# A hybrid decoder block: key norms by products with a block of ones, and one table load by name for each head group

## The chip, the cores and the metric

The kernel runs on one core of a Trainium2 chip. The metric is the device time of one execution in microseconds (us); before the change it is 1561.46, the median of three runs (1561.0 to 1561.86). The core's engines run side by side and wait for each other by semaphores: TensorE (PE) multiplies matrices into PSUM, VectorE (DVE) and ScalarE (ACT) work element by element, GpSimd (POOL) does the same more slowly, and SyncE (SP) starts transfers.

## The reference, cut to what matters

16 meta tokens are put ahead of 256 tokens (272 in all, width 2048, float32). One layer computes RWKV-7 time mixing and FoX attention (16 heads of 64 each) from one projection, merges both by gates, and then applies a SwiGLU network.

```python
proj = xn @ w_in                                  # RWKV, FoX and gate columns
# RWKV, per head of 64:
kk = heads(k * k_k)
kk = kk / jnp.maximum(jnp.sqrt(jnp.sum(kk * kk, axis=-1, keepdims=True)), 1e-12)
y = _wkv7_scan(rh, dh, kh, vh, -kk, kk * ah)      # decay, keys, values, -kk, kk * a
# FoX, per head of 64, _rms being x * rsqrt(mean(x * x) + 1e-6) * gain:
q = _rms(q.reshape(B, L, FOX_HEADS, HEAD_DIM), q_g)
k = _rms(k.reshape(B, L, FOX_HEADS, HEAD_DIM), k_g)
sc = jnp.einsum('bqhd,bkhd->bhqk', q, k) * ATTN_SCALE + forget_bias   # then causal softmax
```

The change concerns the two key norms: `kk` of RWKV, and `k` of FoX.

## The kernel before

All large products are made with float32r operands, each number being split into a high half and the rest: `ACT` copies the raw weights to `wh`, DVE subtracts to get `wl` (`wload`, L322 and L323), and PE multiplies `wh` with both halves of the activations and `wl` with the high half (`mm3`, or `mm2` with two halves side by side). Raw, high and low tiles have four buffers each. A load holds 1024 columns; `run` issues a load and then the products of the load before it.

The heads are worked off in four groups of four heads. A group projects RWKV's `k`, `v` and `r`, makes decay and gate terms from a low-rank product (two Sigmoids of ACT), projects FoX's `q`, `k` and `v`, and then two tiles of the branch gates (`zg`). Features lie on the 128 partitions (two heads, `m` = 0, 1 for the two pairs) and tokens along the free dimension. Everything else of a group (norms, decay, the recurrence over four chunks, the triangular solves in 112 lanes, attention) runs as background streams: Python generators that `yield` the number of nanoseconds of projection after which their next stage is due. `slot` counts projected time and puts one due stage between two k-tiles; the constants at the top (`Y_SQ`, `N_SUM` and the like) are these delays. PE's order is that of the program. For ACT, DVE, POOL and SP the framework arranges the instructions, but for stretches under `manual_schedule`, which keep the program's order.

Key norms before: `head_sums` multiplies the squares (`sq`, stationary) with `bsum`, two columns that mark the two heads, in full float32 (`pe_mm`, L355), so that tokens come to lie on partitions, in three tiles of tokens (128, 128 and 16). DVE puts a floor under the sums and refines a reciprocal root by Newton steps on 12 or 20 columns (`rsqrt_steps`, L259 to L268). `spread` has ACT repeat each root 64 times (L603), and PE transposes the result back to the features' layout (`pe_tr`, L359); DVE multiplies it in. The tiles are `ss` and `kx` in RWKV, `fss` and `fx` in FoX. The query's norm stays in the tokens' layout, since it only scales rows of the scores. RWKV's bonus term already makes a product of the wanted kind: `bs` (L789), the two halves of a split tile against `bones`, a 128x128 block matrix of ones in float32r, whose result has each head's sum on all of its 64 rows.

ACT works with one set of function tables at a time; a load puts another in place. Before, there are two loads in a group: ahead of the Sigmoids (L655), and ahead of the decay's exponentials (L706).

Of the kernel before, what the change touches and what calls it, by code (L numbers as in the profile page):

```python
# [18 lines left out]
P = 128  # L19
# [45 lines left out]
LERP = 2800  # L65
BIAS = 7000
STEP = 1000
NORM = 4200
SUMS = 2000
X_RS = 1400  # L70
X_SPREAD = 1400
X_V = 1900
X_SC = 1600
X_EXP = 1100
X_DIV = 2600
X_PT = 1400
Y_SQ = 1400
Y_SPREAD = 3300
Y_KK = 2900
Y_DECAY = 1400  # L80
Y_AB = 4400
Y_MAT = 2900
Y_NEXT = 2300
Y_BONUS = 1200
# [13 lines left out]
def hybrid_block(ctx, tc, A, out, dbg=None):  # L98
# [69 lines left out]
    xhl = xp.tile([P, KT, 2, L], F32R, tag="xhl", name="xhl")  # L168
    xh, xl = xhl[:, :, 0, :], xhl[:, :, 1, :]
    rsb = xp.tile([P, L], F32, tag="rsb", name="rsb")  # L170


    lo_pool = tc.tile_pool(name="lo", bufs=1, reuse_waits="tile")
# [31 lines left out]
    def zt_(name):  # L205
        return rw.tile([P, 274], F32, tag="z", name=name, bufs=ZB)
# [68 lines left out]
    def rstd1():  # L275
        parts = [et(f"{n}1").bitcast(F32R) for n in ("xqh", "xql")]
        split(*parts, xsum)

        def back():
            ps = aux_ps("rms1")[:, :L]  # L280
            for i in range(4):
                nc.tensor.matmul(ps, allones, parts[i % 2][:, i // 2, :], start=i == 0, stop=i == 3)
            ms = zt_("ms1")[:, :L]
            nc.vector.tensor_scalar(ms, ps, 1.0 / D, RMS_EPS, op0=ALU.mult, op1=ALU.add)
            rt = zt_("rt1")[:, :L]
            rsqrt_small(None, rsb, ms, rt, None)
        return back
# [65 lines left out]
    def pe_mm(out_, lhsT, rhs, start, stop, skip=False):  # L353
        clock[2] += 4 * max(lhsT.shape[-1], rhs.free_size()) / 2.4
        nc.tensor.matmul(out_, lhsT, rhs, start=start, stop=stop, skip_group_check=skip)  # L355
# [223 lines left out]
        nc.vector.tensor_scalar(eps1, rs1, RMS_EPS, None, op0=ALU.mult)  # L579
        gate_done.append(1)  # L580

    def tiles(n):
        return [(n - T, P), (n - P, P)] + ([(0, NMETA)] if n > T else [])

    def head_sums(dst, sqs, n, name):


        ps = aux_ps(name)  # L590
        if n > T:
            nc.gpsimd.memset(dst, 1.0)
        for i, (t0, w) in enumerate(tiles(n)):
            for m in range(2):
                c = 4 * i + 2 * m
                pe_mm(ps[:w, c:c + 2], sqs[m][:, t0:t0 + w], bsum, start=True, stop=True)
        return [(dst[:w, 4 * i:4 * i + 4], ps[:w, 4 * i:4 * i + 4]) for i, (_, w) in enumerate(tiles(n))]

    def spread(rs, m, n, name):

        tl = tiles(n)
        ex = et(name).rearrange("p m t -> p (m t)")[:, :3 * P].rearrange("p (i c) -> p i c", c=P)
        nc.scalar.activation(ex[:, :len(tl), :].rearrange("p i (h d) -> p i h d", h=2),  # L603
                             rs.rearrange("p (i m h) -> p i m h", m=2, h=2)[:, :, m, :].unsqueeze(3).to_broadcast(
                                 [P, len(tl), 2, HD]), AF.Copy)

        def back():
            ps = aux_ps(name)[:, :n]
            for i, (t0, w) in enumerate(tl):
                pe_tr(ps[:, t0:t0 + w], ex[:w, i, :], ident[:w, :w])  # L610
            return ps
        return back


    def rwkv_jobs(g):
        c0 = g * 256
        box = {"done": []}
        for nm in ("k", "v", "r"):
            box[nm] = et(f"{nm}{g}")
        jobs = []  # L620

        def post(nm, off, full):
            def f(pss):
                for m in range(2):
                    mc = vc("mu", off // P + g * 2 + m)
                    dst = box[nm]
                    lerp(pss[m], P, mc, dst[:, m, :] if full else dst[:, m, :T], full, box["done"])
            return f

        for nm, off, full in (("k", 1024, True), ("v", 2048, True), ("r", 0, False)):  # L630
            n0, n = (0, L) if full else (14, T + 2)
            jobs += cm_jobs(w_in[:, off + c0:off + c0 + 256], KT, xhl, n0, n, post(nm, off, full), name=f"{nm}{g}")


        def load():
            cs_ = slice(c0, c0 + 256)
            return wload([(96, 0, [2, 256], [((ALL, 0), A["rwkv_w2"][0][:, cs_]), ((ALL, 1), A["rwkv_a2"][0][:, cs_])]),
                          (P, 512, [2, 256], [((ALL,), kblock(A["rwkv_g2"][0][:, cs_]))])], 1024)

        def mul(w):  # L640
            (uh, ul), (gh, gl) = w
            gg = box["gg"] = ot(f"gg{g}")
            for m in range(2):
                ms = slice(m * P, (m + 1) * P)
                ps = main_ps(f"g{g}{m}")[:, :T]
                for k in range(2):
                    mm3(ps, gh[:, k, ms], gl[:, k, ms], sgh[:, k, :], sgl[:, k, :], k == 0, k == 1)
                nc.vector.tensor_copy(gg[:, m, :], ps)
            for nm, i, dh, dl, bname in (("sig", 0, twh, twl, "w0"), ("aa", 1, adh, adl, "a0")):
                dst = box[nm] = et(f"{nm}{g}")  # L650
                for m in range(2):
                    ms = slice(m * P, (m + 1) * P)
                    ps = (aux_ps if i == 0 else main_ps)(f"{nm}{g}{m}")[:, :L]
                    mm3(ps, uh[:, i, ms], ul[:, i, ms], dh, dl, True, True)
                    nc.scalar.activation(dst[:, m, :], ps, AF.Sigmoid, bias=vc(bname, 2 * g + m))  # L655
            spawn(rwkv_bg(g, box), HOP)
        jobs.append((load, mul))
        return jobs

# [10 lines left out]
    def rwkv_bg(g, box):  # L670
# [14 lines left out]
            nc.scalar.activation(kk[:, m, :], kr[:, m, :], AF.Copy, scale=vi("k_k", m))  # L685
        nc.scalar.activation(sq, kk, AF.Square)
        yield Y_SQ
        kn_ = rw.tile([P, 12], F32, tag="kn", name=f"kn{g}", bufs=2)
        kr_ = rw.tile([P, 12], F32, tag="kn", name=f"kr{g}", bufs=2)
# [5 lines left out]
        for m in range(2):  # L695
            nc.vector.tensor_tensor(kk[:, m, :], kk[:, m, :], backs[m](), op=ALU.mult)
        yield Y_KK

        cs = et(f"cs{g}")
# [279 lines left out]
    def fox_jobs(g):  # L979
# [3 lines left out]
        vv = fx.tile([P, 2, L], F32, tag="vv", name=f"vv{g}", bufs=1)  # L983
        jobs = []
        ready = []
        hs = fx.tile([P, 20], F32, tag="hs", name=f"hs{g}", bufs=4)
        hr = fx.tile([P, 20], F32, tag="hs", name=f"hr{g}", bufs=4)
        done = []

        def sums(sqs, dst, n):  # L990
            c = slice(0, 8) if dst is qn else slice(8, 20)
            for i, (d, ps) in enumerate(head_sums(hs[:, c], sqs, n, f"fss{g}{n}")):
                nc.vector.tensor_scalar(d, ps, 1.0 / HD, eps1[:d.shape[0], i:i + 1], op0=ALU.mult, op1=ALU.add)
            done.append(1)
            return
            yield

        def norms():
            while len(done) < 2:
                yield  # L1000
            yield from rsqrt_steps(fx, hr, hs, [P, 20], "ht")
            yield X_RS

            nc.vector.tensor_tensor(hs[:, 0:8], hs[:, 0:8], hr[:, 0:8], op=ALU.mult)
            backs = [spread(hr[:, 8:20], m, L, f"fx{g}{m}") for m in range(2)]
            yield X_SPREAD
            for m in range(2):
                nc.vector.tensor_tensor(kn[:, m, :], kn[:, m, :], backs[m](), op=ALU.mult)
            yield
            ready.append(1)  # L1010

        def post(dst, n):
            def f(pss):
                sqs = []
                for m in range(2):
                    ps = pss[m]
                    if dst is vv:
                        nc.scalar.activation(dst[:, m, :], ps[:, :n], AF.Copy)
                        continue
                    sq = fx.tile([P, L], F32, tag="sqf", name=f"sqf{g}", bufs=3)  # L1020
                    if dst is qn:
                        halves(dst[:, m, :], ps)
                        nc.scalar.activation(sq[:, :n], dst[:, m, :], AF.Square)
                    else:
                        nc.scalar.activation(sq[:, :n], ps[:, :n], AF.Square)
                        nc.scalar.activation(dst[:, m, :], ps[:, :n], AF.Copy, scale=qk8)
                    sqs.append(sq)
                if dst is vv:
                    spawn(fox_bg(g, qn, kn, vv, hs, hr, ready), HOP)
                else:  # L1030
                    spawn(sums(sqs, dst, n), SUMS)
                    if dst is kn:
                        spawn(norms(), PREP)
# [5 lines left out]
    def fox_bg(g, qn, kn, vv, hs, hr, ready):  # L1039
# [13 lines left out]
        while not ready or not gate_done:  # L1053
# [338 lines left out]
```

## Time and profile before

| | us |
|---|---|
| median of three runs | 1561.46 (1561.0 to 1561.86) |
| the profiled execution | 1561.2 |
| its span, first to last instruction | 1559.5 |
| PE busy | 1552.3 |
| weight loads of PE (PEld) busy | 1365.3 |
| DVE busy | 1013.9 |
| ACT busy | 765.8 |
| POOL busy | 98.5 |

The clock granted to TensorE was 1.000 over the span. In a row of the timeline the first number is the start from the span's first instruction, the second the duration, both in us, and `x12` is the number of instructions in the row; a full-precision product is recorded as two, so six products of `head_sums` are `x12`. Matmuls follow each other before the one ahead has ended, so the time that one takes from the next is read from start to start and not from its duration. In a row of groups the numbers behind the bar are the busy time in us and the mean duration in ns, then the idle time of the engine ahead of it and what ended it. A row of a stretch gives the stretch, its length, the busy time of PE, PEld, DVE, ACT and POOL with their instructions, the clock, the share of the DMA engines and GB/s.

### The profile page before, as it was taken

What the parts mean: (1) busy time and instruction counts of PE and PEld (TensorE: products, weight loads), DVE (VectorE), ACT (ScalarE), POOL (GpSimd) and SP (SyncE); (2) the same over time, 40 slices, a digit from 0 to 9 for tenths busy, and PEclk for the clock granted to TensorE, in tenths of its full rate; (3) what the DMA queues carried; (4) which work ended last, traced back from release to release, by engine and by line L of the source; (5) the groups of instructions that cost most, each with busy time, mean ns of one, the idle gap of its engine ahead of it and who ended that gap; (6) DMA issues with size and microseconds to landing.
All of it is one profiled execution on the core that took longest, in us unless ns stands there. A gap on an engine that the chain in (4) does not pass through costs nothing.

```text
span 1559.5 us, 26189 instructions
## 1 busy us (share of the span) xinstructions
PE 1552.3 (100%) x10225; PEld 1365.3 (88%) x10225; DVE 1013.9 (65%) x1854; ACT 765.8 (49%) x1118; POOL 98.5 (6%) x194
## 2 busy tenths in 40 slices
PE   9999999999999999999999999999999999999998
PEld 9999998989989888999888888888888888888887
DVE  7878688677767856875665666566556666444443
ACT  7655455464555544653544555455445544333332
POOL 2121103102203100000000000000000000000000
PEclk9999999999999999999999999999999999999999
DMA  8656546546644656767566666666666665666663
GB/s 269 179 151 172 158 132 173 159 117 174 172 136 138 182 171 197 245 222 238 181 184 180 189 187 191 187 188 187 187 188 187 187 190 188 188 201 202 185 201 102
DMA packets 211483, 283.33 MB, mean 182 GB/s; under 512 B 23888, under 2 KB 128352, under 8 KB 211360
## 3 DMA queue, kind: packets, MB, share of 16 engines
q1 hardware_dynamic: 206752, 277.53, 60.4%
q10 hardware_dynamic: 4608, 4.13, 0.8%
q8 instruction: 80, 1.31, 0.4%
q14 instruction: 43, 0.35, 0.1%
HBM read 274.43 MB, written 7.19 MB: 181 GB/s over the span
## 4 chain that ended last, share of the span: by engine, by line
PE 95%; DVE 3%; DMA 1%; ACT 1%; issue 1%; SPq 0%; DVEq 0%; ACTq 0%
PE up L392 10%; PE gt L392 10%; PE zg L392 7%; PE dn L1255 5%; PE dn L1254 5%; PE dn L1253 5%; PE up L394 5%; PE gt L394 5%; PE zg L394 3%; PE f L333 2%; PE f L392 2%; PE f L335 2%; PE f L334 2%; PE br L334 2%; PE br L335 2%; PE br L333 2%
## 5 line engine op out<-in xcount | busy, mean ns | idle before, releaser
L323 DVE TENSOR_TENSOR wl<-raw,wh 128x1024 fp32r<-128x1024 f32 (+1 forms) x496 | 603.7, 1218 | 444.4 <-ACT wh L322 443.5
L322 ACT ACTIVATE wh<-raw 128x1024 fp32r<-128x1024 f32 (+1 forms) x496 | 521.2, 1052 | 620.4 <-PE dn L1254 144.5
L392 PE MATMUL gt<-hts,wh 128*128 128x512 f32 x704 | 245.0, 394 | 0.0
L392 PE MATMUL up<-hts,wh 128*128 128x512 f32 x704 | 244.9, 394 | 0.0
L394 PE MATMUL gt<-hts,wl 128*128 128x256 f32 x660 | 186.2, 282 | 0.0
L394 PE MATMUL up<-hts,wl 128*128 128x256 f32 x660 | 186.0, 282 | 0.0
L392 PE MATMUL zg<-xhl,wh 128*128 128x512 f32 x512 | 184.3, 403 | 0.0
L392 PEld LDWEIGHTS up<-hts,wh 128*128 128x128 f32 x704 | 130.1, 188 | 26.5
L392 PEld LDWEIGHTS gt<-hts,wh 128*128 128x128 f32 x704 | 130.1, 188 | 26.4
L1254 PE MATMUL dn<-wh,acl 128*128 128x512 f32 x352 | 139.5, 396 | 0.0
L1253 PE MATMUL dn<-wh,ach 128*128 128x512 f32 x352 | 139.5, 396 | 0.0
L1255 PE MATMUL dn<-wl,ach 128*128 128x512 f32 x352 | 139.5, 396 | 0.0
L394 PE MATMUL zg<-xhl,wl 128*128 128x256 f32 x480 | 135.0, 281 | 0.0
L394 PEld LDWEIGHTS up<-hts,wl 128*128 128x128 f32 x660 | 124.7, 189 | 1.8
L394 PEld LDWEIGHTS gt<-hts,wl 128*128 128x128 f32 x660 | 124.7, 189 | 1.8
L392 PEld LDWEIGHTS zg<-xhl,wh 128*128 128x128 f32 x512 | 94.5, 188 | 20.7 <-issue 1.8
L394 PEld LDWEIGHTS zg<-xhl,wl 128*128 128x128 f32 x480 | 90.6, 189 | 1.1
L1255 PEld LDWEIGHTS dn<-wl,ach 128*128 128x128 f32 x352 | 66.3, 188 | 16.2
L1254 PEld LDWEIGHTS dn<-wh,acl 128*128 128x128 f32 x352 | 66.3, 188 | 16.2
L1253 PEld LDWEIGHTS dn<-wh,ach 128*128 128x128 f32 x352 | 66.3, 188 | 16.1
L333 PE MATMUL f<-xhl,wh 128*128 128x272 f32 x256 | 77.7, 303 | 0.0
L335 PE MATMUL f<-xhl,wl 128*128 128x272 f32 x256 | 73.8, 288 | 0.0
(459 smaller groups left out, 2769.9 us busy)
## 6 DMA issues: line engine op xcount, KB each, us to landing
raw<-in_w_gate_up_dram SPq DMA_DIRECT2D x176, 512.0 KB, 3.7
raw<-in_w_in_dram SPq DMA_DIRECT2D x160, 512.0 KB, 3.8
raw<-in_w_down_dram SPq DMA_DIRECT2D x88, 512.0 KB, 4.7
raw<-in_w_o_dram SPq DMA_DIRECT2D x32, 512.0 KB, 3.8
raw<-in_w_branch_a_dram SPq DMA_DIRECT2D x16, 512.0 KB, 3.8
raw<-in_w_branch_b_dram SPq DMA_DIRECT2D x16, 512.0 KB, 3.7
zgd<-zg ACTq DMA_DIRECT2D x30, 128.0 KB, 2.4
gate<-zgd SPq DMA_DIRECT2D x15, 256.0 KB, 5.3
```

The source lines that it names most:

```text
L322: nc.scalar.activation(wh[:prow, cs_], raw[:prow, cs_], AF.Copy)
L323: nc.vector.tensor_tensor(wl[:prow, cs_], raw[:prow, cs_], wh[:prow, cs_].bitcast(F32), op=ALU.subtract)
L333: nc.tensor.matmul(ps, wh, ah, start=first, stop=False)
L334: nc.tensor.matmul(ps, wh, al, start=False, stop=False)
L335: nc.tensor.matmul(ps, wl, ah, start=False, stop=last)
L392: nc.tensor.matmul(ps.rearrange("p (a t) -> p a t", a=2), wh, act, start=first, stop=last)
L394: nc.tensor.matmul(ps[:, :T], wl, act[:, 0, :], start=False, stop=False)
L1253: nc.tensor.matmul(box[t], ah[:, kt, ts_], wh[:, k, :], start=first, stop=False)
L1254: nc.tensor.matmul(box[t], al[:, kt, ts_], wh[:, k, :], start=False, stop=False)
L1255: nc.tensor.matmul(box[t], ah[:, kt, ts_], wl[:, k, :], start=False, stop=last)
```

## The change

Both key norms are made in the features' layout by `head_norms`. ACT and DVE split the squares into two float32r halves; PE multiplies both with `bones`, four products of 272 columns; DVE puts the floor under the sums (a constant in RWKV; `epsw`, the mean square of the row times 1e-6, in FoX); ACT takes Ln, then Exp with -0.5, which gives the reciprocal root y, and Square, y * y; DVE makes one correction, y * (3 - x * y * y) / 2, and multiplies the keys by it. `epsw` is made once at the start by one more operation of DVE. The roots of FoX use the tile of the attention's bias. The query's norm keeps the old way, now with 8 columns. Behind the Sigmoids of a group the table set that holds both Ln and Exp is loaded by name, and ACT keeps the program's order there. Several delays have new values.

```diff
-NORM = 4200
-SUMS = 2000
+NORM = 6500
+SUMS = 3500
...
-Y_SPREAD = 3300
+N_SUM = 2000
+N_ROOT = 3600
...
-Y_AB = 4400
+Y_AB = 6000
...
+            nc.vector.tensor_scalar(epsw, ms, RMS_EPS, None, op0=ALU.mult)
             rt = zt_("rt1")[:, :L]
             rsqrt_small(None, rsb, ms, rt, None)
...
+    def head_norms(xs, root, dst, floor, name):
+        parts = []
+        for m in range(2):
+            hi, lo_ = (zt_(f"{n}{name}{m}")[:, :L].bitcast(F32R) for n in ("nh", "nl"))
+            split(hi, lo_, xs[m])
+            parts.append((hi, lo_))
+        yield N_SUM
+        pss = []
+        for m in range(2):
+            ps = aux_ps(f"{name}{m}")[:, :L]
+            for i, part in enumerate(parts[m]):
+                clock[2] += L / 2.4
+                nc.tensor.matmul(ps, bones, part, start=i == 0, stop=i == 1)
+            pss.append(ps)
+        for m in range(2):
+            floor(xs[m], pss[m])
+        ys = root()
+        zs = [zt_(f"nz{name}{m}")[:, :L] for m in range(2)]
+        for m in range(2):
+            nc.scalar.activation(ys[m], xs[m], AF.Ln)
+        for m in range(2):
+            nc.scalar.activation(ys[m], ys[m], AF.Exp, scale=-0.5)
+        for m in range(2):
+            nc.scalar.activation(zs[m], ys[m], AF.Square)
+        yield N_ROOT
+        for m in range(2):
+            nc.vector.tensor_tensor(xs[m], xs[m], zs[m], op=ALU.mult)
+            nc.vector.scalar_tensor_tensor(ys[m], xs[m], -3.0, ys[m], op0=ALU.add, op1=ALU.mult)
+            nc.vector.scalar_tensor_tensor(dst[:, m, :], ys[m], -0.5, dst[:, m, :], op0=ALU.mult, op1=ALU.mult)
...
+            with tc.manual_schedule(engines={nc.scalar.engine}):
...
+                nc.scalar.preload_act_table_set("natural_log_exp_and_others")
...
-        for d, ps in head_sums(kn_, [sq[:, m, :] for m in range(2)], L, f"ss{g}"):
-            nc.vector.tensor_scalar(d, ps, 1e-24, None, op0=ALU.max)
-        yield from rsqrt_steps(rw, kr_, kn_, [P, 12], "kt")
-        backs = [spread(kr_, m, L, f"kx{g}{m}") for m in range(2)]
-        yield Y_SPREAD
-        for m in range(2):
-            nc.vector.tensor_tensor(kk[:, m, :], kk[:, m, :], backs[m](), op=ALU.mult)
+        def root():
+            y = et(f"ny{g}")
+            return [y[:, m, :] for m in range(2)]
+        yield from head_norms([sq[:, m, :] for m in range(2)], root, kk,
+                              lambda x_, ps: nc.vector.tensor_scalar(x_, ps, 1e-24, None, op0=ALU.max), f"ss{g}")
...
+        def k_norms(sqs):
+            def root():
+                y = fx.tile([P, 2, L], F32, tag="bias", name=f"fy{g}", bufs=1)
+                return [y[:, m, :] for m in range(2)]
+            yield from head_norms(sqs, root, kn,
+                                  lambda x_, ps: nc.vector.scalar_tensor_tensor(
+                                      x_, ps, 1.0 / HD, epsw, op0=ALU.mult, op1=ALU.add), f"fk{g}")
             ready.append(1)
```

How the instructions stand: PE in the second group, around RWKV's key sums, before. `f_0` and `f_1` are the two halves of FoX's query projection, `rhs` the right-hand side of a chunk of the first group's recurrence.

```order
L392 MATMUL f_1_2595<-xhl,wh 128x512
L394 MATMUL f_1_2595<-xhl,wl 128x256
L355 MATMUL ss_2674<-bsum,sq_2655 128x2 x4
L355 MATMUL ss_2674<-bsum,sq_2655 16x2 x2
L392 MATMUL f_0_2594<-xhl,wh 128x512
L394 MATMUL f_0_2594<-xhl,wl 128x256
```

And with the change (`u` and `y` belong to the same chunk as `rhs`):

```order
L356 MATMUL rhs_2706<-sv_1596,NK_1383 64x64 x4
L393 MATMUL f_1_2605<-xhl,wh 128x512
L395 MATMUL f_1_2605<-xhl,wl 128x256
L393 MATMUL f_1_2605<-xhl,wh 128x512
L395 MATMUL f_1_2605<-xhl,wl 128x256
L393 MATMUL f_1_2605<-xhl,wh 128x512
L395 MATMUL f_1_2605<-xhl,wl 128x256
L393 MATMUL f_0_2604<-xhl,wh 128x512
L395 MATMUL f_0_2604<-xhl,wl 128x256
L607 MATMUL ss_2727<-nhss_2692,bones 128x272
L607 MATMUL ss_2727<-nlss_2693,bones 128x272
L607 MATMUL ss_2730<-nhss_2696,bones 128x272
```

The fourth product, with `nlss_2697`, follows. The sums stood two pairs ahead of `rhs` and now stand four pairs behind it; the six transposes `kx` that came later are gone. Over the program PE has 16 interruptions of the projections by full-precision work fewer.

ACT at the same place, before:

```order
L685 ACTIVATE k_1907<-k_1907,vcol 128x272 x2
L686 ACTIVATE sq_2655<-k_1907 128x544
L322 ACTIVATE wh<-raw 128x1024
L866 ACTIVATE R_2705<-rhs_2700 128x128
L603 ACTIVATE kx_2744<-kr_2673 128x384
L603 ACTIVATE kx_2746<-kr_2673 128x384
L322 ACTIVATE wh<-raw 128x1024
```

And with the change:

```order
L700 ACTIVATE sq_2669<-k_1913 128x544
L323 ACTIVATE wh<-raw 128x1024
L460 ACTIVATE nhss_2692<-sq_2669 128x272
L876 ACTIVATE R_2711<-rhs_2706 128x128
L460 ACTIVATE nhss_2696<-sq_2669 128x272
L323 ACTIVATE wh<-raw 128x1024
L614 ACTIVATE ny_2735<-sq_2669 128x272 x2
L616 ACTIVATE ny_2735<-ny_2735 128x272 x2
L618 ACTIVATE nzss_2736<-ny_2735 128x272
L618 ACTIVATE nzss_2737<-ny_2735 128x272
L399 ACTIVATE qn_2544<-f_0_2604 128x256
```

The two copies of the split stand around `R`, which needs PE's `rhs`; the six activations of the roots stand in one block where the two copies of `kx` were.

SP's queue in the second group, before, from the end of the group's low-rank weights to the second bias transfer:

```order
L318 DMA raw<-in_rwkv_g_dram 128x2x256
L318 DMA raw<-in_w_in_dram 128x4x256
L1064 DMA bias_3372<-ncd 128x544
L318 DMA raw<-in_w_in_dram 128x4x256 x16
L765 DMA d_3125<-NK_2988 32x16x32 x2
L767 DMA d_3125<-NK_2989 32x4x32
L318 DMA raw<-in_w_in_dram 128x4x256
L771 DMA ln_3128<-d_3125 32x1024 x3
L773 DMA ln_3128<-d_3125 4x1024 x4
L318 DMA raw<-in_w_in_dram 128x4x256 x7
L1064 DMA bias_3679<-ncd 128x544
```

And with the change:

```order
L319 DMA raw<-in_rwkv_g_dram 128x2x256
L319 DMA raw<-in_w_in_dram 128x4x256 x17
L775 DMA d_3164<-NK_3032 32x16x32 x2
L777 DMA d_3164<-NK_3033 32x4x32
L319 DMA raw<-in_w_in_dram 128x4x256
L781 DMA ln_3167<-d_3164 32x1024 x3
L783 DMA ln_3167<-d_3164 4x1024 x4
L1069 DMA bias_3355<-ncd 128x544
L319 DMA raw<-in_w_in_dram 128x4x256 x7
L1069 DMA bias_3683<-ncd 128x544
```

The first bias transfer of the group stood 17 weight loads earlier, ahead of the transfers of the lanes (`d`, `ln`), and now stands behind them.

More of the change, by code (lines that the diff above doesn't have):

```diff
@@ L67 @@
 STEP = 1000
-NORM = 4200
-SUMS = 2000
-X_RS = 1400
-X_SPREAD = 1400
+NORM = 6500
+SUMS = 3500
 X_V = 1900
@@ L170, in hybrid_block @@
     rsb = xp.tile([P, L], F32, tag="rsb", name="rsb")
+    epsw = xp.tile([P, L], F32, tag="epsw", name="epsw")
     lo_pool = tc.tile_pool(name="lo", bufs=1, reuse_waits="tile")
@@ L580, in forget_gate, with head_sums @@
         gate_done.append(1)
-    def tiles(n):
-        return [(n - T, P), (n - P, P)] + ([(0, NMETA)] if n > T else [])
-    def head_sums(dst, sqs, n, name):
+    def head_sums(dst, sqs, name):
         ps = aux_ps(name)
-        if n > T:
-            nc.gpsimd.memset(dst, 1.0)
-        for i, (t0, w) in enumerate(tiles(n)):
+        for i in range(2):
             for m in range(2):
                 c = 4 * i + 2 * m
-                pe_mm(ps[:w, c:c + 2], sqs[m][:, t0:t0 + w], bsum, start=True, stop=True)
-        return [(dst[:w, 4 * i:4 * i + 4], ps[:w, 4 * i:4 * i + 4]) for i, (_, w) in enumerate(tiles(n))]
@@ L599, in spread @@
[L599 to L612, printed above, removed]
+                pe_mm(ps[:, c:c + 2], sqs[m][:, i * P:(i + 1) * P], bsum, start=True, stop=True)
@@ new lines, in head_sums @@
+        return [(dst[:, 4 * i:4 * i + 4], ps[:, 4 * i:4 * i + 4]) for i in range(2)]
+    def head_norms(xs, root, dst, floor, name):
[27 more added lines that the diff above has]
+            nc.vector.scalar_tensor_tensor(dst[:, m, :], ys[m], -0.5, dst[:, m, :], op0=ALU.mult, op1=ALU.mult)
@@ L648, in mul @@
                 nc.vector.tensor_copy(gg[:, m, :], ps)
-            for nm, i, dh, dl, bname in (("sig", 0, twh, twl, "w0"), ("aa", 1, adh, adl, "a0")):
-                dst = box[nm] = et(f"{nm}{g}")
-                for m in range(2):
[L652 to L655, printed above, removed]
+            with tc.manual_schedule(engines={nc.scalar.engine}):
+                for nm, i, dh, dl, bname in (("sig", 0, twh, twl, "w0"), ("aa", 1, adh, adl, "a0")):
+                    dst = box[nm] = et(f"{nm}{g}")
+                    for m in range(2):
+                        ms = slice(m * P, (m + 1) * P)
+                        ps = (aux_ps if i == 0 else main_ps)(f"{nm}{g}{m}")[:, :L]
+                        mm3(ps, uh[:, i, ms], ul[:, i, ms], dh, dl, True, True)
+                        nc.scalar.activation(dst[:, m, :], ps, AF.Sigmoid, bias=vc(bname, 2 * g + m))
+                nc.scalar.preload_act_table_set("natural_log_exp_and_others")
             spawn(rwkv_bg(g, box), HOP)
@@ L985, in fox_jobs, with sqf, q_norms @@
         ready = []
[L986 to L1009, printed above, removed]
+        hs = fx.tile([P, 8], F32, tag="hs", name=f"hs{g}", bufs=4)
+        hr = fx.tile([P, 8], F32, tag="hs", name=f"hr{g}", bufs=4)
+        def sqf(m):
+            return fx.tile([P, L], F32, tag="sqf", name=f"sqf{g}{m}", bufs=3)
+        def q_norms(sqs):
+            for i, (d, ps) in enumerate(head_sums(hs, sqs, f"fss{g}")):
+                nc.vector.tensor_scalar(d, ps, 1.0 / HD, eps1[:, i:i + 1], op0=ALU.mult, op1=ALU.add)
+            yield from rsqrt_steps(fx, hr, hs, [P, 8], "ht")
+            nc.vector.tensor_tensor(hs, hs, hr, op=ALU.mult)
+            ready.append(1)
+        def k_norms(sqs):
[5 more added lines that the diff above has]
+                                      x_, ps, 1.0 / HD, epsw, op0=ALU.mult, op1=ALU.add), f"fk{g}")
             ready.append(1)
@@ L1019, in f @@
                         continue
-                    sq = fx.tile([P, L], F32, tag="sqf", name=f"sqf{g}", bufs=3)
+                    sq = sqf(m)
                     if dst is qn:
@@ L1024, in f @@
                     else:
-                        nc.scalar.activation(sq[:, :n], ps[:, :n], AF.Square)
+                        nc.scalar.activation(sq, ps[:, :n], AF.Square)
                         nc.scalar.activation(dst[:, m, :], ps[:, :n], AF.Copy, scale=qk8)
@@ L1030, in f @@
                 else:
-                    spawn(sums(sqs, dst, n), SUMS)
-                    if dst is kn:
-                        spawn(norms(), PREP)
+                    spawn((q_norms if dst is qn else k_norms)(sqs), SUMS)
             return f
@@ L1052, in fox_bg @@
         yield
-        while not ready or not gate_done:
+        while len(ready) < 2 or not gate_done:
             yield X_V
```

3 lines of the change are left out of this document (removed).

## The prediction

> **What bounds the kernel now.** I read the busy shares first, then the chain of waits, then what TensorE waited for.
>
> ```profile
> PE 1552.3 (100%) x10225; PEld 1365.3 (88%) x10225; DVE 1013.9 (65%) x1854; ACT 765.8 (49%) x1118; POOL 98.5 (6%) x194
> PE 95%; DVE 3%; DMA 1%; ACT 1%; issue 1%; SPq 0%; DVEq 0%; ACTq 0%
> ```
>
> The first row alone proves little, because the ends of pipelined matmuls are modelled. The second says that the chain that ended last runs through PE for 95% of the span. The complete list of PE's waits settles it:
>
> ```profile
> PE v L333 <- DVE fl L541: 1.2, 1, 1.2
> PE warmup L296 <- DVE yb L293: 1.1, 1, 1.1
> PE lo L512 <- ACT xhl L242: 0.2, 1, 0.2
> PE lo L335 <- DVE wl L496: 0.2, 1, 0.2
> ```
>
> All four lie in the first 46 us; behind them PE never waits on another engine for a whole matmul step. So PE is a queue that is always full, and an operation costs the steps (start to start) that it puts between two projection matmuls. Weights are far ahead: the load whose low half was finished at 190.84 is first read from that half at 199.93, 9.1 us later (the third load of FoX's query; the PE row is in the next fence). The changed stage is four head groups, some 30 to 640 us; the second, 142 to 269 us, has these busy times (PE, PEld, DVE, ACT, POOL):
>
> ```profile
> 189.62 1.22 DVE L323 TENSOR_TENSOR wl<-raw,wh 128x1024 fp32r<-128x1024 f32 x1
> ...
> 142.45:269.07 126.62, 126.62 (x1112) 115.08 (x1110) 97.19 (x254) 65.53 (x114) 23.83 (x40) 1.00 0.55 153
> ```
>
> **What leaves PE.** Four bursts of full-precision products go from each group: the key sums (`ss`) and their spreading (`kx`) in RWKV, the key half of `fss` and its spreading (`fx`) in FoX. The query's `fss` stays. How each stands between projection matmuls in the second group (start, us, then the matmul):
>
> ```profile
> 198.17 0.40 PE L392 MATMUL f<-xhl,wh 128*128 128x512 f32 x1
> 198.40 0.28 PE L394 MATMUL f<-xhl,wl 128*128 128x256 f32 x1
> 198.52 1.14 PE L355 MATMUL ss<-bsum,sq 128*128 128x2 f32 x12
> 199.59 0.50 PE L392 MATMUL f<-xhl,wh 128*128 128x512 f32 x1
> 199.93 0.28 PE L394 MATMUL f<-xhl,wl 128*128 128x256 f32 x1
> ...
> 208.98 1.07 PE L359 MATMUL kx<-ident,kx 128*128 128x128 f32 x6
> 209.99 0.39 PE L333 MATMUL f<-xhl,wh 128*128 128x272 f32 x1
> 210.22 0.29 PE L334 MATMUL f<-xhl,wh 128*128 128x272 f32 x1
> ...
> 227.00 1.13 PE L355 MATMUL fss<-bsum,sqf 128*128 128x2 f32 x12
> 228.06 0.39 PE L333 MATMUL f<-xhl,wh 128*128 128x272 f32 x1
> ...
> 241.17 1.07 PE L359 MATMUL fx<-ident,fx 128*128 128x128 f32 x6
> 242.17 0.50 PE L392 MATMUL zg<-xhl,wh 128*128 128x512 f32 x1
> ```
>
> A burst costs its own steps and a late second matmul behind it. `ss`: 199.59 - 198.52 = 1.07, and the step from L392 to L394 behind it is 0.34 where it is 0.23 ahead of it, so 0.11 more: 1.18 us. `kx`: 1.01, and behind it a step of 0.23 (209.99 to 210.22) where the steady one of 272 columns is 0.12 (last row of the next fence): 1.12. `fss`: 1.06, and `fx`: 1.00, each with the same 0.11 taken for the refill: 1.17 and 1.11. Together 4.58 us a group, 18.3 us for four.
>
> **What comes to PE.** Two bursts a group of four float32r products with `bones`, 272 columns. The bonus of RWKV makes the same product with 256 columns:
>
> ```profile
> 237.25 0.28 PE L789 MATMUL bs<-rkh,bones 128*128 128x256 f32 x1
> ...
> 237.73 0.29 PE L333 MATMUL f<-xhl,wh 128*128 128x272 f32 x1
> 237.85 0.29 PE L334 MATMUL f<-xhl,wh 128*128 128x272 f32 x1
> ```
>
> Four take 0.48, and the step behind is the usual 0.12: no refill. With 272 columns, 0.48 x 272/256 = 0.51; eight bursts 4.1 us. Net on PE: 18.3 - 4.1 = 14.2 us less. Bounds: a step of 0.12 instead of 0.51/4 = 0.128 makes 3.9 us of the 32 products; if each new burst cost the refill of 0.11 after all, 0.9 more. So 13.3 to 14.4.
>
> **The start.** `epsw` is one more DVE operation ahead of the Newton steps of `rsb`, and the bank that PE waits for (`fl`, first list) is released behind these. A scalar operation of 272 columns there takes 0.29:
>
> ```profile
> 36.72 0.29 DVE L259 TENSOR_SCALAR rsb<-ms 128x272 int32<-128x272 int32 x1
> ```
>
> PE waits already, so 0.3 us of it goes to the end: +0.3 (0 to 0.5).
>
> **ACT and DVE.** Each key norm gives ACT eight activations of 272 columns (two copies, Ln, Exp and Square, two each) for two of 384, and DVE ten operations of 272 (two differences, two floors, six for the correction) for short ones and two products.
>
> ```profile
> L603 ACT ACTIVATE kx<-kr 128x384 f32<-128x384 f32 x8 | 3.7, 509 | 1.6 <-DVE kr L268 1.6
> L1025 ACT ACTIVATE sqf<-f 128x272 f32<-128x272 f32 x8 | 3.1, 388 | 2.3 <-PE f L335 2.3
> L459 ACT ACTIVATE adh<-ad 96x272 fp32r<-96x272 f32 x1 | 0.4, 432 | 0.5 <-DVE ad L448 0.5
> L696 DVE TENSOR_TENSOR k<-k,kx 128x272 f32<-128x272 f32 x8 | 3.2, 432 | 0.7 <-PE kx L359 0.6
> L706 ACT ACT_TABLE_LOAD x4 | 5.1, 1283 | 2.2 <-DVE cs L701 2.1
> ```
>
> Ln, Exp and Square of 272 are not in the trace; I bound them by 0.39 (L1025) and 0.51 (L603, wider) and take 0.43 (L459). ACT: 16 x 0.43 - 4 x 0.51 = +4.8 us a group (4.2 to 6.1). DVE: 20 x 0.43 = 8.7, less four products (1.7) and RWKV's nine Newton steps of 0.17 (1.5; row further down) with a few thresholds: about +5. Over a group of 123 us ACT comes to about 70 us and DVE to about 102: neither becomes the bound, and both lie under PE. Without cover they would cost those 5 us a group, 20 in all. The table load of 1.28 us moves from ahead of the decay's exponentials to right behind the sigmoids; the built order has 14 loads in both programs, so it costs nothing in sum, and ACT's wait ahead of `kx` is gone as well.
>
> The tight place is the new product itself, since PE must find the split there. In the second group ACT copies the second half behind `R`, which waits for PE's `rhs`:
>
> ```profile
> 197.71 0.66 ACT L686 ACTIVATE sq<-k 128x544 f32<-128x544 f32 x1
> ...
> 200.48 0.45 PE L355 MATMUL rhs<-sv,NK 128*64 128x64 f32 x8
> 200.86 0.50 PE L392 MATMUL f<-xhl,wh 128*128 128x512 f32 x1
> ...
> 200.98 0.28 ACT L866 ACTIVATE R<-rhs 128x128 f32<-128x128 f32 x1 [1.32 <-PE rhs L355]
> ...
> 200.01 0.17 DVE L259 TENSOR_SCALAR kr<-kn 128x12 int32<-128x12 int32 x1
> ...
> 210.19 0.78 DVE L696 TENSOR_TENSOR k<-k,kx 128x272 f32<-128x272 f32 x2
> ```
>
> From the matmul behind `rhs` (200.86): `R` ends 0.40 later, the copy takes 0.43, the difference 0.43, some 0.1 for hand-overs: ready after 1.35. PE has four pairs of 0.35 and 0.11 of refill, then three products of 0.13, so it reads the last half after 1.87. Half a microsecond to spare; the squares end (198.37) before that chain. The product is also 2.9 us of projection later in the program than `ss` was. Behind it the floor, the roots and the correction (0.9 + 2.6 + 2.6 us) end before `kx`, its refined root and its product did (from `ss` at 198.52 to the end of `k<-k,kx` at 210.97), so `mat`, 24 us behind, is not later.
>
> The bias transfer of a group's first half now waits for the FoX root, whose tile it reuses, and stands behind the lane transfers in SP's queue. The weight load behind it needs the low half that DVE makes right behind that root, so the queue loses only the issue; the scores that take the bias start at 259.81, and the new product stands about where `fss` was, at 227.0: with 6.1 for the roots and 3.5 for the transfer that leaves POOL over 20 us to prepare it. Cost 0, at most a transfer of 3.5 us a group once, if a weight load ran out:
>
> ```profile
> 259.81 0.90 PE sc L355 x8
> ...
> bias<-ncd SPq DMA_DIRECT2D x8, 272.0 KB, 3.5
> ```
>
> **Sum.** The profiled execution took 1561.2 us (span 1559.5 and 1.7 around it): 1561.2 - 14.2 + 0.3 = 1547.3. The median of the runs shown is 1561.46, 0.26 above it, so the forecast is 1547.6.
>
> **Rivals.**
> Weight loads set PE's pace, not the matmuls. Loads by kind (min/median/max ns):
>
> ```profile
> L355 PEld LDWEIGHTS ss<-bsum,sq x48: 92/190/192, 76.6 to 453.5; 128*128 128x128 f32 x32, 128*16 128x16 f32 x16
> L359 PEld LDWEIGHTS kx<-ident,kx x24: 133/138/143, 84.5 to 463.6; 128*128 128x128 f32 x16, 16*128 16x128 f32 x8
> L789 PEld LDWEIGHTS bs<-rkh,bones x8: 187/188/192, 110.7 to 491.5; 128*128 128x128 f32 x8
> ```
>
> Removed: 32 x 0.190 + 16 x 0.092 = 7.6, twice; 24 x 0.138 = 3.3, twice; added 32 x 0.188 = 6.0. Net -15.8, hence 1561.46 - 15.8 + 0.3 = 1546.0. Against it: the twelve loads of one `ss` add up to 1.9 us in a burst of 1.07, so they overlap. 4%. The Trainium skill (Perfetto Trace Analysis, Identifying the Most-Contended Engine) calls matmul busy time a poor measure of TensorE and the share of weight loading a good one; the -15.8 is what that rule would make of the change.
>
> The splits come late at some of the eight products. If one weight copy (about 1.06 us on ACT) slips ahead of a split, the spare 0.5 is used up and PE waits about 0.5: 4 us in all, 1551.6; a full copy each, 1556. For it: the spare time is small and ACT's order is fixed. 9%.
>
> The gain is taken back by waits for weights, ACT and DVE having more to do. For it: DVE at 97 of 127 us. Against: 9 us of lead. Around 1561: 4%.
>
> Slower: the roots block ACT. At each product six activations stand in one block behind DVE's floor; a weight copy behind them comes after 0.43 + 6 x 0.43 + 1.06, and its low half 1.22 later, 5.3 us, while PE holds a load of 24 products of 0.12, 3.0 us. With no lead PE would wait 2.3 us eight times: 1547.6 + 18 = 1566, slower. It decides only where the lead of 9.1 us has fallen under about 2.3. Also here: a further table load at each root (16 x 1.28), which the built order excludes. 5%.
>
> **How the numbers follow.** The likeliest, 78%: 1547.6, with a range of its own of 1546.5 to 1549.5 from the bounds above. The range reaches down past the weight-load case and up to the late splits: 1545 to 1556. A measurement of this kernel can tell about 0.2% (3.1 us) from no change; faster takes the likeliest, the weight loads and most of the late splits: 0.90; the same 0.05; slower 0.05.
>
> **What would show it.** Right: `kx` and `fx` gone; bursts of four `ss` and `fk` products in steps of 0.12 to 0.13 with no long step behind them; PE's list of waits still with nothing behind 50 us, and its first wait 0.3 longer; the third stage (from the first `zg` of the long run) 14 us earlier and everything behind it of unchanged length. Wrong: waits of PE for `nl` or for `wl`, or weight leads near zero at the roots.

## The result and the profile after

The change takes 1552.13 us (median; 1551.37 to 1553.32) where the kernel before takes 1561.47: a ratio of 0.9943, 95% interval 0.9930 to 0.9956. It is faster by 9.3 us. Forecast were 13.9 us (1547.6, range 1545 to 1556). The profiled execution took 1551.7 us with a span of 1550.0; the spans differ by 9.5 us.

The page of the change, busy time of the engines and the chain that ended last:

```profile
PE 1539.2 (99%) x10113; PEld 1354.0 (87%) x10113; DVE 1027.9 (66%) x1859; ACT 778.6 (50%) x1166; POOL 97.1 (6%) x186
PE 92%; DVE 5%; issue 1%; ACT 1%; DMA 1%; SPq 0%; DVEq 0%; ACTq 0%
```

PE has lost 13.1 us of busy time, but the span only 9.5, and DVE's share of the chain has grown from 3% to 5%. So PE now stands still somewhere. Its list of waits (waiting instruction, what ended the wait, us in total, times, longest) says where; its other rows all lie in the start:

```profile
PE ppt L360 <- DVE s L1103: 4.2, 8, 1.0
```

This row was not there before. `ppt` are the transposes of the attention's probabilities, and `s` is their division by the sums on DVE, the last step of the softmax. The second group as a stretch, and PE at `ss` and `fk` in it:

```profile
139.93:264.63 124.70, 123.38 (x1083) 112.36 (x1082) 100.35 (x254) 68.91 (x125) 22.45 (x39) 1.00 0.54 154
```

```profile
199.81 0.29 PE L607 MATMUL ss<-nhss,bones 128*128 128x272 f32 x1
...
200.30 0.39 PE L393 MATMUL f<-xhl,wh 128*128 128x512 f32 x1
200.53 0.28 PE L395 MATMUL f<-xhl,wl 128*128 128x256 f32 x1
...
228.23 0.29 PE L607 MATMUL fk<-nhfk,bones 128*128 128x272 f32 x1
...
228.72 0.29 PE L334 MATMUL f<-xhl,wh 128*128 128x272 f32 x1
228.85 0.29 PE L335 MATMUL f<-xhl,wh 128*128 128x272 f32 x1
```

The group takes 124.7 us instead of 126.6; forecast were 123. Both bursts take 0.49 (199.81 to 200.30, 228.23 to 228.72), and the step behind them is the usual 0.23 or 0.13: no refill. Then the place of the new wait, first the kernel before, then the change, both in the second group:

```profile
266.93 0.29 PE L394 MATMUL zg<-xhl,wl 128*128 128x256 f32 x1
267.06 0.81 PE L359 MATMUL ppt<-ident,s 128*128 128x128 f32 x4
...
268.28 0.48 PE L392 MATMUL zg<-xhl,wh 128*128 128x512 f32 x1
```

```profile
260.17 0.40 PE L393 MATMUL zg<-xhl,wh 128*128 128x512 f32 x1
261.58 0.41 PE L360 MATMUL ppt<-ident,s 128*128 128x128 f32 x2 [1.02 <-DVE s L1103]
262.29 0.44 PE L360 MATMUL ppt<-ident,s 128*128 128x128 f32 x2 [0.31 <-DVE s L1103]
...
263.14 0.48 PE L393 MATMUL zg<-xhl,wh 128*128 128x512 f32 x1
```

Before, the burst took 1.22 us from its start to the next projection matmul. In the change the matmul ahead is over, by its step of 0.23, at 260.40, and the next one starts at 263.14: 2.74, so 1.52 more. The same reckoning gives 1.45, 1.41 and 0.59 in the first, third and fourth groups, 5.0 us in all. (The expectations below say 5.2; they had not taken off that the matmul ahead is one of 512 columns in some cases and of 256 in others.)

**Where the time went.** All terms by steps of PE, in us: the 16 removed bursts -18.2; the eight new ones +4.4 (seven of 0.49 or 0.50, one of 0.95, the first `ss`); the start -0.9; `ppt` +5.0, and 0.15 at one more burst of it. Sum -9.5, which is the difference of the spans. The -0.9 is no gain of the change: it comes from the moment at which one weight load landed (see the part on the prediction).

### The profile page after: what moved, and what is told of

The parts are those of the page before. It is cut to its first block, busy times and chain, and to the rows that moved or that the text cites. A ratio compares the mean times of both kernels' runs of the same rounds, so it can differ in the third digit from the quotient of the medians.

```text
span 1550.0 us, 26008 instructions
## 1 busy us (share of the span) xinstructions
PE 1539.2 (99%) x10113; PEld 1354.0 (87%) x10113; DVE 1027.9 (66%) x1859; ACT 778.6 (50%) x1166; POOL 97.1 (6%) x186
## 4 chain that ended last, share of the span: by engine, by line
PE 92%; DVE 5%; issue 1%; ACT 1%; DMA 1%; SPq 0%; DVEq 0%; ACTq 0%
PE up L393 10%; PE gt L393 10%; PE dn L1260 5%; PE dn L1259 5%; PE dn L1258 5%; PE zg L393 5%; PE up L395 5%; PE gt L395 5%; PE zg L395 2%; PE f L334 2%; PE f L336 2%; PE f L335 2%; PE br L335 2%; PE br L336 2%; PE br L334 2%; PE f L393 2%
## 5 line engine op out<-in xcount | busy, mean ns | idle before, releaser
L395 PEld LDWEIGHTS up<-hts,wl 128*128 128x128 f32 x660 | 124.7, 189 | 1.8
L395 PEld LDWEIGHTS gt<-hts,wl 128*128 128x128 f32 x660 | 124.7, 189 | 1.8
```

The source lines that it names most:

```text
L395: nc.tensor.matmul(ps[:, :T], wl, act[:, 0, :], start=False, stop=False)
```

## The experiments

**Is the late softmax the missing gain?** One delay is longer, so that `ppt` stands later.

```diff
-X_DIV = 2600
+X_DIV = 4200
```

> The change, with one delay longer: X_DIV from 2600 to 4200, so that the transposes of the softmax (ppt) stand 1.6 us of projection later behind the scores. Theory (late softmax): the trace of the change shows PE waiting for the softmax ahead of ppt in each of the four groups; the stretch from sc to the matmul behind ppt is longer than before by 1.56, 1.63, 1.41 and 0.59 us, 5.2 in all, because DVE begins the softmax 2.7 to 3.5 us behind the start of sc instead of 1.7 to 2.1. With 1.6 us more these waits fall to under 0.2 each, and the time to 1552.1 - 5 = 1547 (1546.3 to 1548.3). Rival (DVE's total work): DVE is the bound of this stretch whatever is read where, and the wait appears again at the next thing that PE reads from DVE or ACT: 1551 to 1553.

Measured: 1547.86 us (1547.08 to 1549.12), ratio 0.9916 (0.9902 to 0.9930). PE's list of waits holds these two rows and one of 0.2 us, all in the start:

```profile
PE warmup L297 <- DVE yb L294: 1.1, 1, 1.1
PE v L334 <- DVE fl L542: 1.0, 1, 1.0
```

The theory's number is met, and the rival falls: DVE's work is the same, and the wait comes back nowhere at its former size (some 1.1 us of it do, at `po`; see the last runs). The kernel before with the same longer delay is the control:

> The kernel before, with X_DIV 4200 instead of 2600, the same delay that took the waits out of the change. Theory (the change made the softmax late): in the kernel before the softmax is late by little, since the stretches of ppt are longer than the shortest by 0.22, 0.43 and 0.43 us; so 1.1 us at most are to be had, ratio 0.9993 (0.9985 to 1.0000). Rival (the longer delay helps any version by about 4 us, by other means than these waits): ratio 0.9974.

Measured: ratio 0.9996 (0.9987 to 1.0005), 1559.88 against 1560.66. The delay helps only where the softmax is late; the change made it late.

**Why is it late?** In the change the lanes' chain on DVE (`lt`, `lx`: the triangular solves) starts beside work of POOL. DVE in the change at the start of the lanes (second group, and one row of the fourth), and POOL in the second group:

```profile
245.65 1.40 DVE L324 TENSOR_TENSOR wl<-raw,wh 128x1024 fp32r<-128x1024 f32 x1 [3.29 <-ACT wh L323]
246.97 0.72 DVE L844 TENSOR_TENSOR lt<-lx,ln 112x31 f32<-112x31 f32 x1
247.73 0.66 DVE L846 TENSOR_TENSOR lx<-lx,lt 112x31 f32<-112x31 f32 x1
248.42 0.19 DVE L844 TENSOR_TENSOR lt<-lx,ln 112x30 f32<-112x30 f32 x1
...
494.76 1.59 DVE L324 TENSOR_TENSOR wl<-raw,wh 128x1024 fp32r<-128x1024 f32 x1 [3.30 <-ACT wh L323]
```

```profile
245.93 1.71 POOL L1074 TENSOR_TENSOR b<-b,cmask 128x256 f32<-128x256 f32 x1
247.60 0.73 POOL L1075 TENSOR_TENSOR bias<-bias,cmask 128x256 f32<-128x256 f32 x1
```

While POOL builds the attention's bias, `lt` takes 0.72 and `lx` 0.66; once POOL is done (248.33) the next takes 0.19. `lt` ends at 247.69 and `lx` at 248.39, each some 0.05 behind an operation of POOL (247.64 and 248.33). The POOL operation beside the weight difference takes 1.71 where the one of the same size behind it takes 0.73. Before, POOL built the bias ten microseconds ahead of the lanes:

```profile
241.63 0.73 POOL L1070 TENSOR_TENSOR bias<-bias,cmask 128x256 f32<-128x256 f32 x1
...
252.22 0.18 DVE L834 TENSOR_TENSOR lt<-lx,ln 112x31 f32<-112x31 f32 x1
```

The bias comes later because its tile now holds the roots of FoX's key norm first. The Trainium skill (SBUF — State Buffer, Who interferes with whom) states that a DVE instruction with two inputs in SBUF contends with a GpSimd instruction that reads SBUF, and calls the ports that the two share an exclusive lock. These rows agree with it: 0.72 for 0.18, 1.71 for 0.73.

So the next run gives the roots a tile of their own:

```diff
-                y = fx.tile([P, 2, L], F32, tag="bias", name=f"fy{g}", bufs=1)
+                y = fx.tile([P, 2, L], F32, tag="fy", name=f"fy{g}", bufs=1)
```

> The change, with the roots of FoX's key norm in a tile of their own instead of the tile of the attention's bias. The transfer of the bias no longer waits for them, and POOL builds the bias some 7 us earlier, as before the change. Theory (late softmax by distance): in three groups POOL's bias overlaps the first 1.4 us of the lanes' chain on DVE, where two operations take 0.72 and 0.66 us instead of 0.18 and 0.19 and a weight difference 1.40 instead of 1.22; without the overlap the softmax begins about 1.1 us earlier in these three groups, and the waits ahead of ppt fall by 0.6 to 1.1 each: 1552.1 - 2.5 = 1549.6 (1548.9 to 1550.5). Rival (the shared tile is the whole cause): all waits ahead of ppt go, 1547. Second rival (DVE's total work): 1552.

Measured: 1548.47 us (1546.65 to 1549.44), ratio 0.9918 (0.9904 to 0.9931). Measured again as the base of the next experiment:

> The change with a tile of their own for the roots of FoX, unaltered, as the base for the run beside it: ratio 0.992 to the kernel before, stretches of ppt 0.1 to 0.7 us longer than the shortest.

1546.74 us, ratio 0.9908 (0.9895 to 0.9922). POOL builds the bias at 216 to 224 us in the second group, and the lanes and `ppt` look like this:

```profile
244.20 1.23 DVE L324 TENSOR_TENSOR wl<-raw,wh 128x1024 fp32r<-128x1024 f32 x1 [3.29 <-ACT wh L323]
245.34 0.18 DVE L844 TENSOR_TENSOR lt<-lx,ln 112x31 f32<-112x31 f32 x1
...
259.67 0.44 PE L360 MATMUL ppt<-ident,s 128*128 128x128 f32 x2 [0.31 <-DVE s L1103]
```

The stretches of `ppt` are 4.7 us shorter than in the change, nearly all of its 5.0. The effect is larger than the 2.5 that I expected, and close to the rival that made the shared tile the whole cause: the slowed operations push the whole chain, and in the fourth group too, where no lane operation is slowed, the weight difference ahead of them is (1.59 instead of 1.23). From the first lane operation to the softmax the chain is 1.0 to 1.3 us shorter than in the change in the first three groups, and 0.3 in the fourth.

Is it POOL's work, or the transfer that comes later, or another order? The last experiment of this row takes the tile of their own and adds only work of POOL, which reads ACT's `BK` and whose result nobody uses. PE, DVE and ACT have the same instructions in the same order.

```diff
+        pz = fx.tile([P, 2, L], F32, tag="fy", name=f"pz{g}", bufs=1)[:, 0, :T]
+        bk_ = BK0.rearrange("p h m d -> p (h m d)")
+        nc.gpsimd.tensor_tensor(pz, bk_, bk_, op=ALU.add)
+        for _ in range(5):
+            nc.gpsimd.tensor_tensor(pz, pz, bk_, op=ALU.add)
         yield Y_TR0
```

> The change with a tile of their own for the roots, and six additions of 256 columns on POOL in each group (0.73 us each by the bias's own row), whose result nobody uses. They wait for ACT's copy BK, about 3 us ahead of the lanes' chain, and so lie where the bias is built in the change; PE, DVE and ACT have the same instructions in the same order as in the run beside it. Theory (POOL beside DVE slows the chain): the first lane operations and the weight difference ahead of them take 0.4 to 0.7 us instead of 0.19, the softmax begins about 1 us later in each group, and PE's waits ahead of ppt grow by about 1 us each: 3 to 4 us more than the run beside it, about 1552. Rival (in the change it was the later transfer or another order of DVE that made the softmax late, not POOL's work): the same time as the run beside it, within 0.7 us.

Measured: 1557.52 us, ratio 0.9977 (0.9968 to 0.9986), 10.8 us more than the run beside it. POOL, DVE and PE's waits in the second group:

```profile
245.37 5.14 POOL L837 TENSOR_TENSOR pz<-pz,BK 128x256 f32<-128x256 f32 x5
...
247.25 0.73 DVE L849 TENSOR_TENSOR lt<-lx,ln 112x31 f32<-112x31 f32 x1
...
262.87 0.41 PE L360 MATMUL ppt<-ident,s 128*128 128x128 f32 x2 [1.85 <-DVE s L1108]
```

The mechanism is shown: POOL's work, with nothing else changed, brings the wait ahead of `ppt` back. The size was missed by a factor of three. The chain from the first lane operation to the softmax is longer by 1.8 to 2.0 us a group, not 1, since POOL's work lasted 5.8 us (244.67 to 250.51) instead of 4.4; and stretches at a lower clock follow, which the last section tells of. In the profiled executions (12.4 us apart) the stretches of `ppt` are 7.9 us longer, and most of the rest lies where the clock is lower. Of the eleven executions, the one whose mean clock was 1.000 took 1553.65.

**Was it also the distance?** From the last `tr` (the transposes ahead of the lanes) to the scores `sc` it was 10.4 to 12.5 us before and 9.4 in the change. The next run puts RWKV's part earlier again:

```diff
-Y_AB = 6000
+Y_AB = 4400
```

> The change, with one delay as it was before: Y_AB 4400 instead of 6000, so that everything of RWKV behind the decay (mat, the transposes tr, the lanes' chain on DVE) stands 1.6 us of projection earlier, and the scores of FoX stay where they are. Theory (late softmax by distance): from the end of tr to sc it was 10.4 to 12.5 us before and is 9.4 with the change, while DVE's chain from the first lane operation to the softmax takes 8.6 to 9.6 us in both; with 1.6 us more distance PE's waits ahead of ppt fall under 0.4 each, 1552.1 - 4.5 = 1547.6 (1546.5 to 1549). If mat then comes before its operands, PE waits there instead, up to 1.6 us a group. Rival (DVE's total work): 1551 to 1553.

Measured: 1551.83 us, ratio 0.9939 (0.9926 to 0.9953): no gain in the whole. By steps, the stretches of `ppt` are 1.7 us shorter than in the change (1.3, 0.5 and 0.2 in the first three groups, 0.5 longer in the fourth); in the profiled execution the first `r` starts 1.8 us later, by the landing of a weight load, and that takes it back. The gain stays small because the scores moved too: the distance grew by 1.0 and not by 1.6, but for the first group, where it is 12.5 again. `tr` was earlier, but in the second group the lanes were not: the weight difference ahead of them in DVE's order waits for ACT's copy and starts only 0.2 us earlier, and takes 0.2 longer beside POOL's bias. The second and the fourth group of this run:

```profile
245.46 1.62 DVE L324 TENSOR_TENSOR wl<-raw,wh 128x1024 fp32r<-128x1024 f32 x1 [2.25 <-ACT wh L323]
247.01 0.72 DVE L844 TENSOR_TENSOR lt<-lx,ln 112x31 f32<-112x31 f32 x1
...
493.61 2.12 POOL L1072 TENSOR_SCALAR bias<-bias,cq,hs 128x272 f32<-128x272 f32 x2
...
495.80 0.69 DVE L844 TENSOR_TENSOR lt<-lx,ln 112x30 f32<-112x30 f32 x1
```

The lanes start at 247.01, as in the change (246.97). And in the fourth group, which had the smallest wait in the change, the lanes now run into POOL: its stretch is 0.5 us longer.

The distance alone is not the cause: the run with a tile of their own has the change's 9.4 in every group, and its stretches of `ppt` are only 0.4 us in all longer than those of the kernel before. POOL's work alone is not either: in the first group of this run `lt` takes 0.72 beside POOL, and with a distance of 12.5 the softmax is in time but for 0.1 us. The change did both. Its chain on DVE from the first lane operation to the softmax is about as long as before (8.6 to 9.6 us, before 8.9 to 9.5), but starts nearer to the scores (5.9 to 6.1 us ahead of them, before 6.8 to 7.6). Without POOL's work it is short enough for that; with it, not.

**What does a product cost?** With the later `ppt`, each new burst is issued twice.

```diff
             for i, part in enumerate(parts[m]):
                 clock[2] += L / 2.4
                 nc.tensor.matmul(ps, bones, part, start=i == 0, stop=i == 1)
+            for i, part in enumerate(parts[m]):
+                nc.tensor.matmul(ps, bones, part, start=i == 0, stop=i == 1)
```

> The change with the transposes of the softmax later (X_DIV 4200, which has no wait ahead of ppt), and each of the eight new bursts issued twice over, eight products of 272 columns instead of four; the second four write the same sums once more. Theory (PE is a full queue, a product costs its step): eight bursts of 0.50 us more, 4.0 us: 1547.9 + 4.0 = 1551.9 (1551.2 to 1552.8), each burst 0.99 to 1.0 us long. Rival (weight loads set the pace: 32 more loads of 0.188): +6.0, 1553.9. Second rival (the bursts stand in slack of PE): no change, 1548.

Measured: 1554.07 us, 6.2 more than with single bursts, which would fit the weight loads' 6.0. The trace says otherwise. A burst of this run, and the first row of its list of PE's waits:

```profile
200.37 0.29 PE L607 MATMUL ss<-nhss,bones 128*128 128x272 f32 x1
...
201.36 0.40 PE L393 MATMUL f<-xhl,wh 128*128 128x512 f32 x1
```

```profile
PE po L356 <- ACT pT L1117: 2.0, 3, 0.8
```

The burst takes 0.99, twice 0.495; all eight together add 3.9 us to PE, as the theory has it. The rest stands at `po`, the products behind `ppt`, which waited for ACT's copies `pT` by 2.0 us in this order; with what the list leaves out, `po` takes 2.8 us more. Why the copies came later in this order stays open. A total that fits a theory would have named the wrong cause here.

**What is the named load worth?**

```diff
-                nc.scalar.preload_act_table_set("natural_log_exp_and_others")
```

> The change without the named load: ACT's tables are loaded where the next function needs them, 32 loads in the program instead of 14, that is two to four more at each of the eight key norms. Theory (ACT lies under PE): 18 x 1.28 = 23 us more on ACT, in pieces of 2.6 to 5.1 us at the roots; mat and sc read the result over 20 us later and weights are 4 us or more ahead, so PE's list of waits gains nothing of its own, and only the waits ahead of ppt move by some tenths: 1552 to 1554. Rival (a load at the roots blocks ACT's weight copies and reaches PE): up to 23 us, 1560 to 1575.

Measured: 1564.41 us, ratio 1.0024 (1.0016 to 1.0033): slower than the kernel before, 12 us more than the change. ACT and DVE at FoX's roots in the second group of this run, and PE behind them:

```profile
230.62 1.28 ACT L614 ACT_TABLE_LOAD   x1
...
238.40 0.44 DVE L621 TENSOR_TENSOR sqf<-sqf,nzfk 128x272 f32<-128x272 f32 x1 [1.66 <-ACT nzfk L618]
...
241.41 0.86 DVE L969 COPY ya<-yT 64x256 f32<-64x256 f32 x2
242.31 0.38 ACT L967 ACTIVATE ya<-yT 64x256 f32<-64x256 f32 x1 [1.50 <-DVE ya L969]
...
242.74 0.66 PE L360 MATMUL trbk<-ident,bk 128*128 128x128 f32 x4 [2.52 <-ACT ya L967]
```

```profile
PE trbk L360 <- ACT ya L967: 7.6, 3, 2.6
```

Four loads stand in this block of roots, which holds ACT from 230.62 to 238.27. DVE's correction waits for the last root (1.66), and in DVE's order its copies of the recurrence's output, `ya`, stand behind the correction and a weight difference. ACT's second copy `ya` waits 1.50 for DVE's, and PE's transposes `trbk` wait 2.5 us for it, in three groups (the last row, from PE's list of waits). These waits are 7.6 of the 12.4 us between the profiled executions; two stretches at half clock (last section) can make up to 3.4 more. The time lies in the rival's range, but by another way: the wait for weights that I had named for it does not appear. My expectation of 1552 to 1554 was wrong: cover for the weight copies is not cover for everything that waits for the roots, on ACT or on DVE.

**The change once more, and both remedies together.**

> The change itself, unaltered, on the same chip as the three beside it, so that these are compared with it and not across chips. Expected: ratio to the kernel before 0.994, PE waiting ahead of ppt for 4.2 us in its list of waits (1.56, 1.63, 1.41 and 0.59 us longer stretches than before). What is open: whether the start, which was 0.86 us earlier than before at the first r of the first group, comes out of the order (then it is the same here) or out of the landing of a weight load (then it moves by up to 1 us).

Measured: 1551.69 us, ratio 0.9944 (0.9932 to 0.9957); `ppt` waits 4.2 us again. The first `r` starts 1.07 us earlier than in the profile before, against 0.86 in the first profile of the change.

> The change with both remedies, X_DIV 4200 and a tile of their own for the roots of FoX. Theory (late softmax): with the later transposes alone no wait ahead of ppt is left, so the second remedy has nothing more to take: the same as the first alone, 1547.9 (1547 to 1549.2). Rival (the tile of its own also frees something else, a queue or POOL): a further 1 us or more, 1546.5 or less.

Measured: 1545.91 us (1545.78 to 1546.06), ratio 0.9906 (0.9891 to 0.9921), the best of all versions and 5.8 us under the change beside it. That is 1 us below the range of my theory, where the rival had put it: with the later `ppt` alone something was left that no list of waits shows. `po` there and with both remedies, second group:

```profile
264.39 1.03 PE L356 MATMUL po<-pT,vt 128*64 128x256 f32 x6
...
265.71 0.39 PE L334 MATMUL k<-xhl,wh 128*128 128x272 f32 x1
```

```profile
263.74 0.92 PE L356 MATMUL po<-pT,vt 128*64 128x256 f32 x8
...
264.69 0.39 PE L334 MATMUL k<-xhl,wh 128*128 128x272 f32 x1
```

1.32 us against 0.95 from its start to the next projection matmul. In the first, ACT's second `pT` ends at 264.73, in the middle of the burst. Over all bursts that is 1.1 us.

## Why the prediction was right, and what it missed

- **PE is a full queue, and what leaves it is gained.** Right. The removed bursts were forecast at 18.3 us and made 18.2.
- **The new products.** Forecast 0.51 a burst without refill; measured 0.49 to 0.50. Only the first `ss` took 0.95, since its halves came late (DVE made the lower ones at 78.15, behind a weight difference, and PE began at 78.28): the "late splits" rival, at one place of eight. (The 1.87 in the prediction's check of the splits is 1.90 by its own terms; nothing hangs on it.)
- **The start.** Forecast +0.3, measured -0.9. The operation that makes `epsw` did take 0.21, but the weight difference ahead of it started a microsecond earlier in this execution, behind a weight load that landed earlier. The kernel before and the change, DVE:

```profile
35.57 1.23 DVE L323 TENSOR_TENSOR wl<-raw,wh 128x1024 fp32r<-128x1024 f32 x1 [1.91 <-ACT wh L322]
```

```profile
34.57 1.23 DVE L324 TENSOR_TENSOR wl<-raw,wh 128x1024 fp32r<-128x1024 f32 x1 [0.99 <-ACT wh L323]
35.72 0.29 DVE L285 TENSOR_SCALAR epsw<-ms 128x272 f32<-128x272 f32 x1
35.93 0.29 DVE L259 TENSOR_SCALAR rsb<-ms 128x272 int32<-128x272 int32 x1
```

  From the start of this weight difference to the first `r` it is 20.27 us in both profiled executions without `epsw` (35.57 to 55.84 in the kernel before; the other is the control) and 20.40 to 20.43 in all ten with it (34.57 to 54.98 in the change). So the operation costs some 0.14, within the 0 to 0.5 of the prediction. The rest is when the load lands, and that varies: the difference starts between 34.36 and 36.38 in the ten. The microsecond gained there is luck.
- **The bias transfer, "cost 0".** This is the step that failed. I had asked whether the bias would be ready for the scores, and it was, by 4.8 us (248.33 against 253.10), not by over 20. The product does not stand where `fss` was: it starts 24.9 us ahead of the scores (228.23 against 253.10), where `fss` stood 32.8 ahead (227.0 against 259.81). The transfer is issued at 236.38, behind the lanes' transfers, and POOL begins after some other work:

```profile
236.38 0.35 SPq L1069 DMA_DIRECT2D bias<-ncd  x1
...
243.97 0.90 POOL L1072 TENSOR_SCALAR b<-bias,cq,hs 128x144 f32<-128x144 f32 x2
```

  I had not asked what else runs at the time to which POOL's work moves, nor that the lanes would start nearer to the scores. Beside the lanes' chain POOL makes DVE late, and the softmax waits in DVE's queue. With the roots in a tile of their own 4.7 us of 5.0 come back. The signs that I had named for a miss (waits for `nl` or `wl`) did not appear; PE's list of waits had the row all the same.
- **ACT and DVE hidden under PE.** Right on average (100.4 us of DVE and 68.9 of ACT in the second group's 124.7), and in the case of the weights. The share of a group was no measure for the 17 us from 245.65 to the end of the softmax (262.67), in which DVE is busy for 16.5 us, with no pause over 0.05.
- **The result** lay at the place of the late splits (1551.6), for another reason: a stretch of PE that waits for DVE, four times. That the range held the result is so far luck: no rival named this wait. With the wait removed the kernel takes 1545.9 to 1548.5 in four runs, which is about where the likeliest case stood.

## What to carry to other kernels

When a tile is shared and a transfer moves, follow what the transfer sets off, not only whether it arrives in time: the engine that works on its data may now run beside another one and slow it down. A share of busy time says nothing about a stretch in which an engine never idles, so look at each chain that ends in the bound engine's queue, and at its distance. And where an edit's total fits a theory, look up its terms: here 6.2 us were 3.9 of products and a wait.

## What the runs showed of the hardware

**The clock can fall behind waits of TensorE under 3 us.** In the run with POOL's added work and in the one without the named load, PE's waits were followed by stretches of 3.41 us at half clock. The first two rows are such stretches, one of each run (behind the waits of 1.85 and of 2.5 in the second group); the third, of the run without the named load, lies behind the wait of 2.5 in its third group. The columns are busy times, the granted clock, the DMA share and GB/s:

```profile
264.64:268.05 3.41, 3.41 (x14) 2.77 (x14) 3.27 (x8) 1.41 (x4) 3.41 (x6) 0.50 0.61 171
```

```profile
243.73:247.14 3.41, 3.41 (x15) 2.86 (x14) 3.38 (x7) 1.67 (x3) 2.31 (x2) 0.50 0.88 269
...
371.60:376.00 4.40, 4.39 (x30) 3.91 (x31) 4.37 (x8) 3.94 (x8) 2.29 (x2) 1.00 0.83 239
```

3.41 us at half clock cost at most 1.7 us, about as much as the wait of 1.85 itself. It happened in three of four groups of the first run and in two of three places of the second; behind the change's own waits of 1.0 and 0.3 the clock stayed at 1.00. Transposes stand at each of these waits, so I also counted from the end of the last other matmul's step to the next other matmul. In the twelve profiled executions, behind the start, the five falls followed stretches of 3.1 to 3.6 us, one stretch of 3.1 had none, and the thirteen of 2.2 to 2.8 had none. The Trainium skill (TensorE: Matmul & The Clock Gate, Why this matters for your kernels) advises against gaps of more than about 3 us; these stretches agree with that if transposes count into the gap. By the waits alone, added up at each place, falls came from 1.7 us on and 1.4 us had none; that is far less than 3, and no run here tells the two countings apart.

**DVE and POOL slow each other by whole instructions.** `lt` of 31 columns takes 0.18 us alone and 0.72 beside POOL, and ends as POOL's operation ends; an operation of POOL of 256 columns takes 0.73 alone and 1.71 beside a weight difference of DVE.
